# The inverse's results move into the preparation's buffers, and the merge's copies are split between two engines

## The chip, the cores and the metric

The kernel runs on one core of one Trainium2 chip, in one launch. The metric is the device time of a run in microseconds (us). The core's engines are TensorE (PE, with its weight loads apart as PEld), VectorE (DVE), ScalarE (ACT), GpSimd (POOL) and SyncE (SP). Each works through its own list in a fixed order. SP and POOL here mostly issue DMA transfers, in order too.

## The reference

Two layers over 512 latent tokens of width 1024, with 256 context tokens ahead of them. Layer 0 is a bidirectional RWKV-7 recurrence beside a gated short convolution, layer 1 a convolution module. Only the recurrence of layer 0 is touched:

```python
def wkv_scan(S0, r, decay, k, v, kk, a, reverse):
    def step(S, inp):
        r_t, w_t, k_t, v_t, kk_t, a_t = inp
        sa = jnp.einsum("bhvk,bhk->bhv", S, -kk_t)
        S = (S * w_t[:, :, None, :]
             + sa[..., None] * (kk_t * a_t)[:, :, None, :]
             + v_t[..., None] * k_t[:, :, None, :])
        return S, jnp.einsum("bhvk,bhk->bhv", S, r_t)
    S, out = lax.scan(step, S0, (r, decay, k, v, kk, a), reverse=reverse)
    return out, S
...
yac, S_f, S_b = rwkv_seq(rwkv_prep(hc, rc, kc, vc, *rw), zero, zero, r_k, lnx_w, lnx_b, ctx_out)
...
ya, _, _ = rwkv_seq(rwkv_prep(h, r, k, v, *rw), S_f, S_b, r_k, lnx_w, lnx_b, True)
yb = bg * dwconv(cg * xb, sc_w, seg_len)
```

There are 16 heads of 64, both directions, first over the context (whose final states S_f and S_b start the latent scan), then over the latent tokens.

## The kernel before

The scan is done in chunks of 64 tokens. Inside a chunk the dependence of a token on the tokens before it is a unit triangular 64x64 system, one for each head, chunk and direction; its inverse is computed once and then applied by matmuls while the state walks from chunk to chunk.

The work comes in 12 stages, called here c0 to c3 (context, two pairs of heads each, 4 chunk steps) and l0 to l7 (latent, one pair each, 8 chunk steps in both directions). Stage s runs its **chain** (`chain_ctx` or `chain_lat`, the steps from chunk to chunk, each a handful of small matmuls on PE, copies on ACT and, on DVE, the new state H). What belongs to later stages is prepared beside it, in the order that the strings in `STAGE` give; each letter is a part of the program:

- P: projections r, k, v of stage s+2 (big 128x512 matmuls), L: `light`, elementwise work of stage s+2 on DVE and ACT, for direction z=0 and then z=1, in the single buffers `kd`, `a` and `P`;
- H: `heavy` of stage s+2: the triangular blocks (`pa`, masked by DVE into tile E, L601), their copy into `Nt` by ACT (L618), transposes `pb` copied to BKt (L612) and values `pv` copied to UV (L629);
- S: `solve` of stage s+1: DVE transposes `Nt` into X (L650), and runs 31 pairs of operations on X and Y (L656, L658) that invert all 32x32 diagonal blocks. Y is loaded with the unit matrix by a DMA of the POOL queue;
- F, C, O: gate projections, the end of the stage, the short convolution (`conv_branch`) and one product per stage.

The 64x64 inverse is **merged** from the 32x32 ones at the end of `solve`: DVE transposes Y into R1 (L661) and R1 into R2 (L662); ACT copies R1 into E (four copies, L667); PE makes pg, ACT copies it to Gs (L676); PE makes px, ACT copies it into E (L681). R1 is stored in `Nt`, R2 in Y and Gs in X. There is one buffer of each of these, so the next `heavy` can write `Nt`, and the next `solve` can start, only after the merge has read them. The merged part of E is first read in step 0 of the stage's chain (PE, uh<-Ol,E).

All engines' orders are static. They come from a list scheduler that goes by the order in which the program is written, with anchors: `light` and `heavy` are held behind given steps of the chain in progress (`LIGHT_AFTER`, `HEAVY_AFTER`). The big matmuls of projections and gates are spread between the small ones of the chains. Their weights are loaded by SP into two raw buffers, cast by ACT (wh, L126), and DVE makes the remainder (wl, L127). SP also stores the final state of a context chain (h0d<-Hc, L724), between weight loads.

In names, the number is the pair or stage (l4: latent pair 4), and wr, wh and wl are the raw weights, their cast and the remainder.

Of the kernel before, what the change touches and what calls it, by code (L numbers as in the profile page):

```python
# [15 lines left out]
P = 128  # L16
# [15 lines left out]
CONV_AFTER = (0, 2, 7, 6)  # L32
PA_ORDER = ((0, 1), (1, 0), (1, 1), (0, 0))
HEAVY = ("VBOAN", "ANBV")
STAGE = ("OFPLSH", "OSPLHFC")
FILL_R = (0, 0, 2, 3, 4, 4, 4, 4)
FILL_Z = (0, 1, 1, 1, 3, 3, 3, 3)
ZR = (slice(0, 64), slice(64, 128))
# [13 lines left out]
def kernel(ctx: ExitStack, tc: tile.TileContext, I: dict, out: bass.AP):  # L52
    nc = tc.nc
    V, S, G, T = nc.vector, nc.scalar, nc.gpsimd, nc.tensor

    def mm(o, lhsT, rhs, start, stop):
        return T.matmul(o, lhsT, rhs, start=start, stop=stop)  # L57
# [98 lines left out]
    l0, rs = ExitStack(), ExitStack()  # L156
# [20 lines left out]
    def w(tag, name, dt=F32):  # L177
        return wk.tile([P, SIZE.get(tag, 512)], dt, tag=tag, name=name, bufs=NBUF.get(tag, 1))

    def ch3(t, x=CH):  # L180
        return t.rearrange("p (c x) -> p c x", x=x)

    def small(name, shape):
        return cvp.tile(shape, F32, tag=name, name=name)
# [11 lines left out]
    Nt = small("Nt", [P, 16, 32])  # L196
# [196 lines left out]
    def prep_ctx(b, between=None):  # L393
        st = state(False, b)
        for which in (1, 2):
            st["rkv"[which]] = t = w("rkv"[which] + "_", "rkv"[which] + st["nm"])
            for p, cs in st["parts"]:
                project(p, which, t[:, cs])
                if between:
                    between()  # L400
        return st
# [240 lines left out]
    def solve(st):  # L642
        nm, E = st["nm"], st["E"]
        Xt = w("X", "X" + nm)
        X = Xt.rearrange("p (a b) -> p a b", b=32)
        Yt = w("Y", "Y" + nm)
        Y = Yt.rearrange("p (a b) -> p a b", b=16)
        tmp = w("xtmp", "xtmp" + nm)
        nc.gpsimd.dma_start(Y, I["unit"])
        V.transpose(X.rearrange("p (r s) t -> p t r s", r=2),  # L650
                    Nt.rearrange("p q t -> p t q").unsqueeze(2).to_broadcast([P, 32, 2, 16]))
        for i in range(31, 0, -1):
            c0 = i // 2
            m = 16 - c0
            tv = tmp[:, : i * m].rearrange("p (a b) -> p a b", b=m)
            V.tensor_tensor(out=tv, in0=X[:, :i, i : i + 1].to_broadcast([P, i, m]),  # L656
                            in1=Y[:, i : i + 1, c0:].to_broadcast([P, i, m]), op=ALU.mult)
            V.tensor_tensor(out=Y[:, :i, c0:], in0=Y[:, :i, c0:], in1=tv, op=ALU.add)  # L658
        R1 = Nt
        R2 = Yt.rearrange("p (a b) -> p a b", b=32)  # L660
        V.transpose(R1.rearrange("p q (c r) -> p c r q", r=2), Y.rearrange("p (a b) c -> p c a b", a=2))  # L661
        V.transpose(R2, R1)  # L662
        Gs = Xt[:, 0:512].rearrange("p (a b) -> p a b", b=32)
        for z in range(2):
            for b in range(2):
                rs = slice(64 * z + 32 * b, 64 * z + 32 * b + 32)
                S.copy(E[rs, 1 - z, :, 32 * b : 32 * b + 32], R1[rs])  # L667
        pg = px = uhs[1]
        top = [slice(64 * z, 64 * z + 32) for z in range(2)]
        low = [slice(64 * z + 32, 64 * z + 64) for z in range(2)]  # L670
        for q in range(16):
            for z in range(2):
                mm(pg[low[z], q * 32 : q * 32 + 32], E[top[z], 1 - z, q, 32:64], R2[top[z], q, :],
                   True, True)
        for z in range(2):
            S.copy(Gs[low[z]], ch3(pg[low[z]], 32))  # L676
        for q in range(16):
            for z in range(2):
                mm(px[top[z], q * 32 : q * 32 + 32], Gs[low[z], q, :], R1[low[z], q, :], True, True)
        for z in range(2):  # L680
            S.copy(E[top[z], 1 - z, :, 32:64], ch3(px[top[z]], 32))  # L681

    cmm = pinned()

# [176 lines left out]
    def rest(n=1):  # L861
        for g in range(mv["n"], min(mv["n"] + n, 16)):
            half_, kt = g // 8, g % 8
            if kt == 0:
                mv["acc"] = uhs[0] if half_ == 0 else ps.tile([P, 512], F32, tag="zo", name="mpb", bufs=2)
                V.memset(mv["acc"], 0.0)
            for q in range(4):
                u = 4 * half_ + q
                layer, c0 = (0, 2 * D + 512 * u) if u < 2 else (1, 512 * (u - 2))
                if g < 2:  # L870
                    with tc.issue_after(env["last"].ins):
                        nc.sync.dma_start(mws[q], I["mod_w"][layer, kt * P : (kt + 1) * P, c0 : c0 + 512])
                    continue
                nc.gpsimd.dma_start(mws[q], I["mod_w"][layer, kt * P : (kt + 1) * P, c0 : c0 + 512])
            for q in range(4):
                mm(mv["acc"][32 * q : 32 * q + 2, :], s2[:, kt, :], mws[q], kt == 0, kt == KT - 1)
            if kt == KT - 1:
                rested(half_, mv["acc"])
        mv["n"] += n

    def rested(half_, acc):
        row = w("HP", f"mrow{half_}")
        mt = ps_at(f"mr{half_}")
        for b in range(2):
            S.copy(row, acc[:, 256 * b : 256 * b + 256])
            for j in range(2):
                T.transpose(mt[:, (2 * b + j) * P : (2 * b + j + 1) * P], row[:, j * P : (j + 1) * P], ident)
        src = mt.rearrange("p (j q x) -> p q j x", j=4, q=4)[:, :, :, 0]
        for dst, u0, n, bias in (((gate0, 0, 2, col("mod_b0", 16, 8)), (modc1[:, 0:8], 2, 2, col("mod_b1", 0, 8)))
                                 if half_ == 0 else ((modc1[:, 8:24], 0, 4, col("mod_b1", 8, 16)),)):  # L890
            V.tensor_tensor(out=dst.rearrange("p (q j) -> p q j", q=n), in0=src[:, u0 : u0 + n],
                            in1=bias.rearrange("p (q j) -> p q j", q=n), op=ALU.add)
        if half_ == 0:
            V.memset(acc, 0.0)
# [9 lines left out]
    sts = [prep_ctx(0, rest)]  # L904
# [3 lines left out]
    heavy(sts[0])  # L908
    rest()
    solve(sts[0])  # L910
    rest(2)
    sts.append(prep_ctx(1, rest))
    light(sts[1])
# [2 lines left out]
    for s in range(12):  # L916
        st = sts[s]
        if s < 4:
            for i in range(NCTX):
                chain_ctx(st, i)  # L920
        else:
            for i in range(NLAT):
                chain_lat(st, i)
        if s == 11:
            finish(st)
            break
        for x in STAGE[s >= 4]:
            if x == "S":
                solve(sts[s + 1])
            elif x == "O":  # L930
                if sts[s + 1]["lat"]:
                    sts[s + 1]["po"]()
            elif x == "P" and s < 10:
                sts.append(prep_ctx(s + 2) if s < 2 else prep_lat(s - 2))
            elif x == "L" and s < 10:
                light(sts[s + 2], st)
            elif x == "H" and s < 10:
                heavy(sts[s + 2], st)
            elif x == "F":
                fills(s + 1)  # L940
                if s >= 4:
                    finish(st)
            elif x == "C":
                conv_branch(s - 3, st["anchor"])
                if s == 10:
                    rs.close()
                    op = rs.enter_context(tc.tile_pool(name="op", bufs=1, reuse_waits="tile", side="right"))
                    env["lo"] = V
        if s == 3:
            G.memset(cx[:, :, 0:66:65], 0.0)  # L950
            conv_branch(0)
            V.scalar_tensor_tensor(out=gsc1, in0=modc1[:, 8:16], scalar=1.0, in1=col("g_pre1", 0, 8),
                                   op0=ALU.add, op1=ALU.mult)
            gv = ss6
            V.tensor_tensor(out=gv[:, 0:8], in0=gate0, in1=col("g_post", 0, 8), op=ALU.mult)
            V.tensor_tensor(out=gv[:, 8:16], in0=modc1[:, 16:24], in1=col("g_post", 8, 8), op=ALU.mult)
            pgv = ps_at("pgv")
            T.transpose(pgv[:16, :P], gv, ident)
            gvr = w("xtmp", "gvr")[0:16, 0:P]
            S.copy(gvr, pgv[:16, :P])  # L960
            nc.sync.dma_start(gvd.rearrange("a (k p) -> (a k) p", p=P), gvr)
# [26 lines left out]
    with ExitStack() as l1:  # L988
# [118 lines left out]
        for n in range(4):  # L1107
            ws = {}
            for part, tag in ((1, "wa"), (0, "wb")):
                for kt in range(0, KT, 2):  # L1110
# [3 lines left out]
                    w = split(src, f"wc{n}{part}{kt}", tag)  # L1114
# [3 lines left out]
            for m in range(4):  # L1118
# [10 lines left out]
                a = lt("a", f"a{n}{m}")  # L1129
# [20 lines left out]
        for j in range(16):  # L1150
# [5 lines left out]
            t = t2[:, j % 2 * 512 : j % 2 * 512 + 512]  # L1156
# [4 lines left out]
        for j in range(16):  # L1161
# [10 lines left out]
            t = lt("wb" if j < 10 else "xr", f"y{j}", F32R)  # L1172
# [12 lines left out]
        for n in range(2):  # L1185
# [17 lines left out]
            for m in range(4):  # L1203
# [3 lines left out]
                t = lt("a", f"sq{m}{n}") if n else None  # L1207
# [93 lines left out]
```

## Time and profile before

| | before |
|---|---|
| three runs, median | 1486.42 us (1476.52 to 1487.33) |
| the profiled execution | 1487.99 us, of which span 1486.2 us |
| PE busy | 1421.5 us (96%) |
| DVE busy | 955.8 us (64%) |
| ACT busy | 777.6 us (52%) |
| mean granted clock of TensorE | 0.976 of full |

The span is the time from the first to the last recorded instruction; the profiled execution has 1.8 us around it. Context stages lie in about the first 470 us after the start, latent stages from there to about 990 us, and the output projection and layer 1 take the rest, which the change does not touch. A latent stage repeats every 61.8 us (the transposes into R1, L661, start at 649.63, 711.40, 773.21 and 835.16 us).

### The profile page before, as it was taken

Reading aid. Unit: us, or ns where it says so; the run is one execution under the profiler, and the core shown is the slowest. Engines: PE = TensorE matmul, PEld = TensorE weight load, DVE = VectorE, ACT = ScalarE, POOL = GpSimd, SP = SyncE. Lnnn points to the kernel's source line nnn. Section 1 sums busy time; section 2 is a strip of 40 time slices with the busy share of each in tenths; the row PEclk is TensorE's granted clock in tenths of the full one; section 3 lists DMA queues with packets and bytes.
Section 4 is the critical chain, followed back from the end, with each engine's and each line's share of the span. In section 5 each row is a group of like instructions: output and inputs, shape, how many; then the busy total and the mean of one; then the engine's idle time right before and its main releaser. Section 6 shows DMA issues by size and latency. Waiting matters only on the chain.

```text
span 1486.2 us, 29753 instructions
## 1 busy us (share of the span) xinstructions
PE 1421.5 (96%) x11921; PEld 1015.5 (68%) x11921; DVE 955.8 (64%) x2250; ACT 777.6 (52%) x1564; POOL 128.5 (9%) x250
## 2 busy tenths in 40 slices
PE   6899999999999999999999999999889999999998
PEld 1464667878767666666666666677767777688876
DVE  2665576668696978888788787657545535544333
ACT  4536364374755575755757556546544313463222
POOL 2022210000110101011010100011100000000000
PEclk9999997999996999999999999999989999999999
DMA  8754431312232312231222213358603203133322
GB/s 324 216 168 161 154 110 58 103 58 75 74 104 65 90 60 79 62 94 45 86 73 59 90 30 100 131 201 304 208 30 114 86 28 113 46 97 99 98 87 85
DMA packets 137627, 158.55 MB, mean 107 GB/s; under 512 B 15375, under 2 KB 104143, under 8 KB 137369
## 3 DMA queue, kind: packets, MB, share of 16 engines
q1 hardware_dynamic: 121104, 106.47, 23.0%
q0 software_dynamic: 15312, 48.99, 10.3%
q8 instruction: 94, 1.54, 0.4%
q10 hardware_dynamic: 1072, 1.19, 0.2%
q14 instruction: 45, 0.37, 0.1%
HBM read 138.33 MB, written 18.28 MB: 105 GB/s over the span
## 4 chain that ended last, share of the span: by engine, by line
PE 47%; ACT 7%; DVE 5%; issue 1%; DMA 1%; DVEq 0%; SPq 0%; ACTq 0%
PE pu L57 12%; PE f L57 6%; PE pz L57 6%; PE o L57 4%; PE zol L57 3%; PE pbg L57 3%; PE pxb L57 3%; PE uh L57 2%; PE pal L57 1%; PE pc L57 1%; PE px L57 1%; PE pcg L57 1%; ACT Nt L618 1%; DVE E L601 1%; ACT UV L629 1%
## 5 line engine op out<-in xcount | busy, mean ns | idle before, releaser
L57 PE MATMUL o<-wh,y 128*128 128x512 f32 x248 | 80.2, 401 | 1.0 <-ACT wh L126 1.0
L57 PE MATMUL pal<-ARl,BKl 64*128 64x128 f32 x512 | 59.1, 311 | 6.9 <-DVE xtmpc L656 4.3
L658 DVE TENSOR_TENSOR Yl<-Yl,xtmpl 128x126 f32<-128x126 f32 (+22 forms) x248 | 61.9, 250 | 2.2
L656 DVE TENSOR_TENSOR xtmpl<-Xl,Yl 128x126 f32<-128x126 f32 (+22 forms) x248 | 61.9, 249 | 2.0
L57 PEld LDWEIGHTS pal<-ARl,BKl 64*128 64x128 f32 x512 | 44.2, 199 | 26.4 <-DVE E L601 6.1
L1136 ACT CAST ah<-a 64x512 fp32r<-64x512 f32 x32 | 19.8, 618 | 72.9 <-DVE a L1131 72.5
L57 PE MATMUL zol<-UV,E 64*64 64x64 f32 (+1 forms) x1024 | 54.2, 221 | 0.0
L57 PEld LDWEIGHTS o<-wh,y 128*128 128x128 f32 x248 | 46.7, 191 | 10.9 <-ACT wh L126 1.1
L57 PE MATMUL o<-wl,y 128*128 128x512 f32 x124 | 50.3, 405 | 3.9 <-DVE wl L127 3.9
L57 PE MATMUL zol<-Hl,ARl 64*64 64x64 f32 x896 | 50.2, 230 | 1.9 <-DVE Hl L769 1.9
L762 ACT COPY UV<-uh 64x128 f32<-64x128 f32 x128 | 33.4, 261 | 33.4 <-PE uh L57 31.1
L601 DVE TENSOR_TENSOR E<-pal,maskE 128x512 f32<-128x512 f32 x64 | 43.4, 683 | 11.0 <-PE pal L57 10.9
L127 DVE TENSOR_TENSOR wl<-wr,wh 128x1024 fp32r<-128x1024 f32 x28 | 37.0, 1320 | 20.9 <-ACT wh L126 20.7
L57 PEld LDWEIGHTS zol<-Hl,ARl 64*64 64x64 f32 x896 | 35.1, 133 | 20.7 <-issue 16.8
L769 DVE SCALAR_TENSOR_TENSOR Hl<-uh,PCl,HPl 128x64 f32<-128x64 f32 x112 | 26.6, 279 | 30.6 <-PE uh L57 22.6
L57 PEld LDWEIGHTS uh<-UV,BKt 128*64 128x64 f32 x704 | 26.8, 138 | 28.0 <-ACT UV L762 21.6
L57 PEld LDWEIGHTS zol<-UV,E 64*64 64x64 f32 (+1 forms) x1024 | 42.4, 136 | 2.8 <-ACT UV L762 2.1
L1131 DVE TENSOR_TENSOR a<-pu,a 128x512 f32<-128x512 f32 x16 | 11.0, 689 | 51.3 <-PE pu L57 49.0
L1092 DVE SCALAR_TENSOR_TENSOR pr<-px,dbe,What 119x512 f32<-119x512 f32 x32 | 22.5, 746 | 32.8 <-PE px L57 32.7
L126 ACT CAST whcg<-wrcg 128x512 fp32r<-128x512 f32 x16 | 9.9, 619 | 64.0 <-DMA wrcg<-in_ev_w_in_dram 60.1
L126 ACT CAST wh<-wr 128x1024 fp32r<-128x1024 f32 x28 | 29.4, 1049 | 23.5 <-PE o L57 11.0
L57 PE MATMUL uh<-UV,BKt 128*64 128x64 f32 x704 | 37.0, 234 | 4.0 <-ACT UV L762 2.5
(935 smaller groups left out, 4306.5 us busy)
## 6 DMA issues: line engine op xcount, KB each, us to landing
wr<-in_ev_w_out_dram SPq DMA_DIRECT2D x28, 512.0 KB, 5.4
mwo<-in_mod_w_dram POOLq DMA_DIRECT2D x28, 256.0 KB, 3.3
mwr<-in_mod_w_dram POOLq DMA_DIRECT2D x28, 256.0 KB, 4.2
ectx<-in_mod_w_dram SPq DMA_DIRECT2D x12, 512.0 KB, 5.1
wrk<-in_ev_w_in_dram SPq DMA_DIRECT2D x16, 256.0 KB, 2.8
wrv<-in_ev_w_in_dram SPq DMA_DIRECT2D x16, 256.0 KB, 3.7
wrr<-in_ev_w_in_dram SPq DMA_DIRECT2D x16, 256.0 KB, 2.9
wrza<-in_ev_w_in_dram SPq DMA_DIRECT2D x16, 256.0 KB, 2.8
```

What stands on the lines that cost most here:

```text
L57: return T.matmul(o, lhsT, rhs, start=start, stop=stop)
L126: S.copy(hi, raw)
L127: env["lo"].tensor_tensor(out=lo, in0=raw, in1=hi, op=ALU.subtract)
L601: V.tensor_tensor(out=E[:, h, z * NLAT + c0 : z * NLAT + c0 + m, :], in0=pas[h], in1=maskE[:, z * (1 + h) : z * (1 + h) + 1, 0:x].to_broad ...
L618: S.copy(Nt[rs], E[rs, h, :, 32 * b : 32 * b + 32])
L629: S.copy(dst, src if lat or not z else src[:, :, ::-1, :])
L656: V.tensor_tensor(out=tv, in0=X[:, :i, i : i + 1].to_broadcast([P, i, m]), in1=Y[:, i : i + 1, c0:].to_broadcast([P, i, m]), op=ALU.mult)
L658: V.tensor_tensor(out=Y[:, :i, c0:], in0=Y[:, :i, c0:], in1=tv, op=ALU.add)
L762: u_ = S.copy(UV[ZR[1 - h], i : 2 * nch - i : 2 * nch - 1 - 2 * i, ZR[h]], uh[ZR[1 - h], 0:2, :])
L769: h_ = V.scalar_tensor_tensor(out=Hn[:, z, :], in0=uh[:, 2 + z, :], scalar=PC[z][:, i : i + 1], in1=HP[:, z, :], op0=ALU.mult, op1=ALU.add)
L1092: V.scalar_tensor_tensor(out=pr[s][:NPROD], in0=px[s][:NPROD], scalar=dbe[:, 0:1], in1=What[:, n * 512 : n * 512 + 512], op0=ALU.add, op1= ...
L1136: S.copy(ahl[s][hr], a[hr])
```

## The change

The merge becomes a function of its own, `merge`, with a letter M of its own. R1, R2 and Gs no longer lie in `Nt`, Y and X, but in the buffers `kd`, `a` and `P` of `light`. So `Nt`, Y and X are free once the solve's own last operations are through; and the merge of stage s+1 has to come after `light` of stage s+2 is through with those three buffers, while the next `light` has to come after the merge. In `STAGE`, M stands behind L and S, and ahead of H. Of the eight copies of a merge, ACT keeps four and DVE gets four. Instructions on PE, and the DMAs, are the same in number.

```diff
-STAGE = ("OFPLSH", "OSPLHFC")
+STAGE = ("OFPLSMH", "OSPLMHFC")
...
-        R1 = Nt
-        R2 = Yt.rearrange("p (a b) -> p a b", b=32)
+        st["Y"] = Y
+
+    def merge(st):
+        nm, E, Y = st["nm"], st["E"], st["Y"]
+        R1, R2, Gs = (w(t, f"{t}m{nm}")[:, 0:512].rearrange("p (a b) -> p a b", b=32) for t in ("kd", "a", "P"))
         V.transpose(R1.rearrange("p q (c r) -> p c r q", r=2), Y.rearrange("p (a b) c -> p c a b", a=2))
         V.transpose(R2, R1)
-        Gs = Xt[:, 0:512].rearrange("p (a b) -> p a b", b=32)
         for z in range(2):
             for b in range(2):
                 rs = slice(64 * z + 32 * b, 64 * z + 32 * b + 32)
-                S.copy(E[rs, 1 - z, :, 32 * b : 32 * b + 32], R1[rs])
+                (V.tensor_copy if b else S.copy)(E[rs, 1 - z, :, 32 * b : 32 * b + 32], R1[rs])
...
         for z in range(2):
-            S.copy(Gs[low[z]], ch3(pg[low[z]], 32))
+            (V.tensor_copy if z else S.copy)(Gs[low[z]], ch3(pg[low[z]], 32))
...
         for z in range(2):
-            S.copy(E[top[z], 1 - z, :, 32:64], ch3(px[top[z]], 32))
+            (V.tensor_copy if z else S.copy)(E[top[z], 1 - z, :, 32:64], ch3(px[top[z]], 32))
...
     solve(sts[0])
+    merge(sts[0])
...
             if x == "S":
                 solve(sts[s + 1])
+            elif x == "M":
+                merge(sts[s + 1])
```

The order moves in three places of interest. In the order, R1 is called kdm (the buffer kd used by the merge), R2 am and Gs Pm.

The first is ACT between chains l3 and l4, from the merge of l4 to the first scaled output of chain l4 (Ol4, copied from zol4_0). Before:

```order
L667 COPY E100_4343<-Nt_112 32x16x32 x4
L676 COPY Xl4_8086<-uh1_124 32x512 x2
L618 COPY Nt_112<-E110_5045 32x512 x2
L629 COPY UV110_5044<-pvl5_8419 64x8x64 x2
L681 COPY E100_4343<-uh1_124 32x16x32 x2
L618 COPY Nt_112<-E110_5045 32x512 x2
L629 COPY UV110_5044<-pvl5_8419 64x8x64 x2
L789 ACTIVATE gzb4_8634<-pzb4_8609 128x512
L756 COPY Ol4_8642<-zol4_0_8643 128x128
```

And after:

```order
L669 COPY E100_4355<-kdml4_8277 32x16x32 x2
L678 COPY Pml4_8279<-uh1_124 32x512
L683 COPY E100_4355<-uh1_124 32x16x32
L126 CAST whcg50_9336<-wrcg50_9335 128x512
L618 COPY Nt_112<-E110_5060 32x512 x4
L612 COPY BKt110_5061<-pbl500_8406 128x8x64
L612 COPY BKt110_5061<-pbl501_8407 128x8x64
L126 CAST whcg51_9342<-wrcg51_9341 128x512
L612 COPY BKt111_5062<-pbl511_8427 128x8x64
L612 COPY BKt111_5062<-pbl510_8426 128x8x64
L629 COPY UV110_5059<-pvl5_8446 64x8x64 x4
L126 CAST whxb50_9375<-wrxb50_9374 128x512
```

The merge's copies are four in place of eight and stand together ahead of all copies of stage l5's heavy, with whose Nt and UV they were interleaved. Right behind the last row of after come the gate's gzb4 and Ol4, as before.

The second is DVE in the context part, around the state after step 0 of chain c1 (Hc1_0) and the transpose that begins solve c2 (Xc2). Before:

```order
L717 TENSOR_SCALAR Hc1_0_2885<-uh0_123,PCc10_1691 128x64 x2
L717 TENSOR_SCALAR Hc1_0_2885<-uh0_123,PCc11_1721 128x64 x2
L127 TENSOR_TENSOR wlk70_3173<-wrk70_3171,whk70_3172 128x512
L601 TENSOR_TENSOR ectx_121<-pac2001_2842,maskE_108 128x512
L601 TENSOR_TENSOR ectx_121<-pac2000_2841,maskE_108 128x512
L601 TENSOR_TENSOR ectx_121<-pac2101_2862,maskE_108 128x512
L601 TENSOR_TENSOR ectx_121<-pac2100_2861,maskE_108 128x512
L650 STREAM_TRANSPOSE Xc2_3476<-Nt_112 128x32x32
L719 SCALAR_TENSOR_TENSOR Hc1_1_2923<-uh0_123,PCc10_1691,HPc1_0_2918 128x64 x2
```

And after:

```order
L669 COPY ectx_121<-kdmc1_2709 32x16x32 x2
L369 SCALAR_TENSOR_TENSOR lr2_3101<-plr2_3076,hmu_101,lr2_3101 128x511
L127 TENSOR_TENSOR wlk61_3115<-wrk61_3113,whk61_3114 128x512
L678 COPY Pmc1_2711<-uh1_124 32x512
L127 TENSOR_TENSOR wlk70_3179<-wrk70_3177,whk70_3178 128x512
L601 TENSOR_TENSOR ectx_121<-pac2000_2847,maskE_108 128x512
L601 TENSOR_TENSOR ectx_121<-pac2001_2848,maskE_108 128x512
L683 COPY ectx_121<-uh1_124 32x16x32
L601 TENSOR_TENSOR ectx_121<-pac2101_2868,maskE_108 128x512
L601 TENSOR_TENSOR ectx_121<-pac2100_2867,maskE_108 128x512
L650 STREAM_TRANSPOSE Xc2_3482<-Nt_112 128x32x32
L719 TENSOR_SCALAR Hc1_0_2891<-uh0_123,PCc10_1694 128x64 x2
```

The merge of c1 now stands here (it was some 50 rows earlier, ahead of light c2), and Hc1_0 has moved from ahead of heavy c2's masks to behind Xc2, the place where Hc1_1 was. It is the same with merge c2 and Hc2_0 around Xc3. On SP, the stores of h0d from chains c1 and c2 stay ahead of the weight loads wrr30 and wrr50.

The third is PE at the seam from context to latent, ahead of the second half of the triangular blocks of l0 (pal010 and pal011, of direction z=1). Before:

```order
L57 MATMUL plr5_4689<-hlh_118,whr51_4684 128x512
L57 MATMUL plr5_4689<-hll_119,whr51_4684 128x512
L57 MATMUL plr6_4731<-hlh_118,whr60_4720 128x512
L57 MATMUL plr6_4731<-hll_119,whr60_4720 128x512
L57 MATMUL pal0101_4359<-ARl01_4194,BKl01_4195 128x128
```

And after:

```order
L57 MATMUL plr5_4701<-hlh_118,whr51_4696 128x512
L57 MATMUL plr5_4701<-hll_119,whr51_4696 128x512
L57 MATMUL plr5_4701<-hlh_118,wlr51_4697 128x512
L57 MATMUL plr5_4701<-hlh_118,whr51_4696 128x512
L57 MATMUL plr5_4701<-hll_119,whr51_4696 128x512
L57 MATMUL plr5_4701<-hlh_118,wlr51_4697 128x512
L57 MATMUL plr5_4701<-hlh_118,whr51_4696 128x512
L57 MATMUL plr5_4701<-hll_119,whr51_4696 128x512
L57 MATMUL plr5_4701<-hlh_118,wlr51_4697 128x512
L57 MATMUL pal0101_4371<-ARl01_4203,BKl01_4204 128x128
```

With the rows ahead of these, 13 big matmuls of plr5 now stand in a row ahead of pal010, where there were four (two of plr5 and two of plr6).

## Rows read from the trace of the kernel before

**Rows 1.** The page: busy time, share of the span, instructions.

```profile
PE 1421.5 (96%) x11921; PEld 1015.5 (68%) x11921; DVE 955.8 (64%) x2250; ACT 777.6 (52%) x1564; POOL 128.5 (9%) x250
```

**Rows 2.** Windows, two latent stages: us, busy per engine, clock, DMA share, GB/s.

```profile
630.00:692.00 62.00, 59.29 (x774) 40.15 (x774) 51.39 (x154) 40.08 (x95) 7.01 (x13) 1.00 0.25 71
692.00:754.00 62.00, 59.27 (x776) 40.19 (x776) 51.27 (x154) 40.07 (x94) 6.93 (x14) 1.00 0.24 71
```

**Rows 3.** Waits of PE, 692 to 754 us: total, times, longest.

```profile
PE uh L57 <- ACT Ol L756: 0.9, 1, 0.9
PE pzb L57 <- DVE wlzb L127: 0.5, 1, 0.5
...
```

**Rows 4.** Timeline of ACT around merge l4: start, us, instruction, idle before.

```profile
712.53 2.52 ACT L667 COPY E<-Nt 32x512 f32<-32x512 f32 x4 [1.13 <-DVE Nt L661]
715.07 1.17 ACT L676 COPY Xl<-uh 32x512 f32<-32x512 f32 x2
...
718.71 1.17 ACT L681 COPY E<-uh 32x512 f32<-32x512 f32 x2
...
722.83 0.26 ACT L756 COPY Ol<-zol 128x128 f32<-128x128 f32 x1
```

**Rows 5.** Timeline of DVE around the same merge.

```profile
711.40 1.10 DVE L661 STREAM_TRANSPOSE Nt<-Yl 128x512 f32<-128x512 f32 x1
...
721.16 2.01 DVE L650 STREAM_TRANSPOSE Xl<-Nt 128x1024 f32<-128x1024 f32 x1 [1.77 <-ACT Nt L618]
```

**Rows 6.** Groups by line, shapes apart, DVE: busy us, mean ns, idle before.

```profile
L601 DVE TENSOR_TENSOR E<-pal,maskE 128x512 f32<-128x512 f32 x64 | 43.4, 683 | 11.0 <-PE pal L57 10.9
...
L259 DVE TENSOR_SCALAR tok<-tok,ss 128x1024 f32<-128x1024 f32 x6 | 4.5, 753 | 0.2
```

**Rows 7.** Timeline of PE, big matmuls and then a small one.

```profile
705.06 0.40 PE L57 MATMUL pzb<-hll,whzb 128*128 128x512 f32 x1
705.29 0.39 PE L57 MATMUL pzb<-hlh,wlzb 128*128 128x512 f32 x1
705.61 0.27 PE L576 MATMUL pbl<-ident,BKl 64*128 64x64 f32 x1
```

**Rows 8.** Windows of the context part, columns as in rows 2.

```profile
200.00:215.00 15.00, 14.80 (x199) 10.92 (x195) 11.36 (x19) 14.78 (x31) 1.08 (x2) 1.00 0.23 72
215.00:240.00 25.00, 23.80 (x140) 17.66 (x141) 8.78 (x12) 9.87 (x19) 1.07 (x2) 0.59 0.22 64
372.00:384.00 12.00, 12.00 (x192) 9.08 (x193) 9.05 (x21) 9.06 (x19) 4.53 (x8) 0.72 0.37 113
...
440.00:453.00 13.00, 7.47 (x102) 6.00 (x101) 12.19 (x25) 5.12 (x9) 1.66 (x3) 0.74 0.34 101
453.00:470.00 17.00, 17.00 (x159) 12.77 (x156) 4.43 (x10) 7.58 (x15) 0.54 (x1) 0.50 0.12 33
```

**Rows 9.** Waits of PE, 430 to 480 us.

```profile
PE pal L57 <- DVE xtmpc L656: 4.3, 1, 4.3
PE uh L57 <- DVE Yc L662: 1.2, 1, 1.2
```

**Rows 10.** Waits of PE, 200 to 240 us.

```profile
PE plr L57 <- ACT whr L126: 1.2, 1, 1.2
```

**Rows 11.** Timeline of DVE in chain c1: states Hc and the transpose into Xc.

```profile
321.86 0.85 DVE L717 TENSOR_SCALAR Hc<-uh,PCc 128x64 f32<-128x64 f32 x4
...
332.98 2.03 DVE L650 STREAM_TRANSPOSE Xc<-Nt 128x1024 f32<-128x1024 f32 x1 [2.46 <-ACT Nt L618]
334.89 0.83 DVE L719 SCALAR_TENSOR_TENSOR Hc<-uh,PCc,HPc 128x64 f32<-128x64 f32 x4
340.39 0.85 DVE L719 SCALAR_TENSOR_TENSOR Hc<-uh,PCc,HPc 128x64 f32<-128x64 f32 x4
```

**Rows 12.** Timeline of SP's queue at the end of chain c2.

```profile
418.66 1.19 SPq L724 DMA_DIRECT2D h0d<-Hc  x2
419.99 8.90 SPq L123 DMA_DIRECT2D wrr<-in_ev_w_in_dram  x4
```

## Prediction

> **What bounds the kernel now.** I read the page's shares first: PE is busy 96% of the span, DVE 64% and ACT 52% [rows 1]. An average hides stages, so next came the windows. Two successive latent stages look alike: of 62.00 us PE is busy 59.3, DVE 51.3 and ACT 40.1, at full clock [rows 2]. So PE is the bound there; some 2.7 us of a stage are left in which it idles. The waits of PE in one such stage give them names: 0.9 us on ACT's Ol (the first scaled output of a chain), 0.5 on a weight remainder of DVE, the rest in smaller pieces [rows 3]. No wait for the merge itself is among them. In the timeline of ACT the reader sees why Ol is late: from 712.53 us on ACT works without a gap through the merge's copies (2.52, 1.17 and 1.17 us) and those of the next heavy, and reaches Ol at 722.83 [rows 4]. In the context part PE loses more: a wait of 4.3 us for light l0 and 1.2 us for a merge's transposed result [rows 9], 1.2 us for a weight cast behind a full ACT [rows 8, 10], and above all stretches at half clock. At 0.50, the lower of the two levels (1.2 GHz), stand the 17 us from 453 to 470 us; from 215 to 240 us the mean is 0.59, from 372 to 384 us it is 0.72 [rows 8].
>
> **The price of what is moved.** Per merge ACT loses two copies of R1 (2.52/4 = 0.63 us each) and two of PSUM (1.17/2 = 0.585 each): 2 x 0.63 + 2 x 0.585 = 2.4 us [rows 4]. DVE gets these four. The trace has no 32-partition copy on DVE. The nearest rows for a PSUM source are the masks of L601 at 0.683 us for 512 elements; for an SBUF source the scaling of L259, with one source too, takes 0.753 us for 1024, so a 512-element copy lies between 0.38 and 0.683 [rows 6]. The sum is 2 x 0.683 + 2 x 0.38 to 0.683 = 2.1 to 2.7 us per merge; I take 2.3. DVE goes from 51.3 to 53.6 of 62 us, and the 8.4 us left hide it. If that cover were gone, each stage would pay up to 2.7 us.
>
> **Latent stages, seven merges l1 to l7.** The merge moves to an earlier place, and next to it the copies no longer stand among those of Nt and UV. What is removed between Nt and the next solve (Nt, X and Y free early) shortens a DVE wait of 1.77 us [rows 5], which is not on PE's path. What PE can win is its wait on Ol. In the new order ACT still passes four Nt copies, four of BKt, four of UV and the gate ahead of Ol, but 2.4 us less of merge, four of whose copies are done much earlier. The wait can shrink by all of its 0.9 us or by nothing; a weight cast (whxb50) now stands ahead of the gate and Ol, so I take half, 0.45 x 7 = -3.2 us (0 to -6.3).
>
> Against this goes PE's own order. Big matmuls follow each other after 0.23 us, a small one follows a big one after 0.32 [rows 7]: 0.09 us more at a change between kinds. Counted in the order, the changes per stage from pair 0 to 6 go from 61, 61, 63, 63, 63, 63, 53 to 63, 61, 65, 69, 69, 65, 49: +14 in all, 14 x 0.09 = +1.3 us (0 to +3, if the change back costs as much again). And the merge's own matmuls and the bonus product (waiting for the scaled output of the stage before, which on DVE now stands behind the next X of 2.01 us [rows 5]) can bring new waits: 0 to 0.5 us a stage; I take 0.1, +0.7 in all (0 to +3.5). Latent sum: -3.2 + 1.3 + 0.7 = -1.2 us, from -6 to +6.
>
> **The seam from context to latent.** The 4.3 us wait [rows 9] belongs to pal010, which needs the last of light l0. The order puts 13 big matmuls ahead of it where four stood: 9 x 0.23 = 2.1 us of work fall into the gap [rows 7], -2.1 us. Bounds: 0 (if the weights of these matmuls come late) and -4.3. The merge c3 goes behind light l0, which DVE works on here without a gap; its chain starts some rows later, and its 1.2 us wait stays. Weight remainder wlr51 and the four copies also stand on DVE here: I price them at nothing, since PE then has the plr5 matmuls.
>
> **c0 and ACT.** From 200 to 215 us ACT is busy 14.78 of 15.00, with merge c0 in it [rows 8]. Minus 2.4 us of copies, the 1.2 us wait for whr behind it [rows 10] should go: -1.2 us (0 to -1.2).
>
> **Chains c1 and c2.** Their merges now wait for light's last use of the three buffers. Hc1_0 was at 321.86, Hc1_1 behind Xc2 at 334.89, the following step at 340.39 [rows 11]; with Hc1_0 behind Xc2, the chain is one step late, 340.39 - 334.89 = 5.5 us, and chain c2 likewise. PE has projections to fill with, so 0 us; the upper bound is the whole step for both, +11 us. Queued behind are SP's stores of h0d and, in order behind these, weight loads: at chain c2's end the store at 418.66 is followed at 419.99 by four loads wrr [rows 12].
>
> **The sum.** -1.2 - 2.1 - 1.2 = -4.5 us against the profiled execution's 1487.99, so 1483.5. That execution lies 1.6 us above the median of the three runs, 1486.42; against the median the sum gives **1482 us**. The half-clock stretches I leave as they are. In this forecast the terms' own bounds give about 1473 to 1493.
>
> **Rival 1: the clock comes back.** One stretch of half clock began in the gap of 4.3 us: 440 to 453 us, with that gap in it, has a mean of 0.74, and 453 to 470 us 0.50, which costs 13 x 0.26 + 17 x 0.50 = 11.9 us at most (some of the first part is idle anyway). The stretch of 215 to 240 us began after the wait of 1.2 us and costs 25 x (1 - 0.59) = 10 us [rows 8]. If filling the gap, or taking the 2.4 us from ACT, keeps the clock up, the time is 1482 - 12 = 1470 for the first, with both 1460. For it: both stretches start at an idle spot that the change shortens. Against it: from 372 to 384 us PE is busy all of 12.00 us, and the clock still fell to a mean of 0.72 [rows 8], amid the merge's small matmuls, so idle time is not the only thing that brings it down. The Trainium skill, TensorE: Matmul & The Clock Gate, Part 1 (The HAM clock gate), has the clock throttled by default and after an idle stretch, and released by activity; by that rule the shortened gap would win these 12 us, and the stretch of 372 to 384 us, with no idle in it, does not bear the rule out in full.
>
> **Rival 2, slower: late chains starve PE of weights.** Chain c2 ends 5.5 us later, so the store of h0d goes at about 424 and the four loads of wrr come as much later. Those of them that belong to pair 5 feed the 13 matmuls now ahead of pal010. PE would then stand for up to those 5.5 us in place of the gap saved, and a longer idle spell is paid again in clock: another stretch like that of 453 to 470 us, 8.5 to 12 us, at c2 or earlier. It gives 1482 + 2 + 5.5 + 8.5 to 12, about 1498 to 1502. It decides from the point where wrr51's cast is later than plr5's turn. For it: SP's order is strict, and DVE is full at this place. Against it: these loads spread over 8.90 us [rows 12] because they wait for buffers, which does not shift with the store.
>
> **Rival 3: no effect.** The wait on Ol merely becomes one on another copy, since ACT's list up to Ol is as long in the end, and at the seam light l0 ends later by DVE's added work, 2.3 us, which eats the 2.1 gained. Then 1486. Also here: DVE at 53.6 of 62 is no bound, but where it is full already the copies cost.
>
> **How the numbers follow.** Chances: the forecast 0.45; rival 1 0.25 (one stretch 0.15, both 0.10); rival 2 0.15; rival 3 0.15. About 1% (15 us) is what a measurement of this kernel can tell from no change, as its three runs lie 11 us apart. Faster by over 1% is below 1471.6: both stretches (0.10), two thirds of the cases with one (0.10), and the best end of the forecast (0.04): 0.24. Slower by over 1% is above 1501.3: the worse half of rival 2 and its combination with bounds elsewhere: 0.12. Within: 0.64. The range leaves out the lower half of rival 1's two-stretch case and the upper part of rival 2: 1461 to 1499.
>
> **What would show it.** In the profile after: PE's wait on Ol at 0 to 0.9 per latent stage, the transposes into R1 still 61 to 62 us apart; DVE about 53.6 of 62 in such a stage, ACT 37.7; the copies on DVE at 0.38 to 0.68 us. At the seam a wait of pal of about 2 us in place of 4.3, and the same length of half clock behind it. The wait for whr near 215 us gone. Hc1_0 behind Xc2, some 13 us later than before, with no idle of PE around it. A stage period off by more than 1 us, or a half-clock stretch that is gone or new, would make the prediction wrong.

## The result, and the profile after

The changed kernel took 1469.74 us in the median of eight runs (1465.69 to 1473.59), the kernel before 1486.88 (1476.52 to 1494.88). The ratio is 0.9902, 95% interval 0.9875 to 0.9929: 17 us, some 1.2%, less in the difference of the medians. The profiled execution took 1470.48 us, with a span of 1468.7. Forecast were 4.4 us, with 1482 us in a range of 1461 to 1499.

The page after, busy time and share of the span (1468.7 us):

```profile
PE 1417.8 (97%) x11921; PEld 1014.3 (69%) x11921; DVE 987.8 (67%) x2298; ACT 749.9 (51%) x1516; POOL 128.4 (9%) x250
```

Against [rows 1] PE's busy time is 3.7 us less; the other 13.8 us of the span's 17.5 are idle time of PE that went. The mean granted clock is 0.978 after 0.976, so over the whole execution the clock gives almost nothing, though it moves in single stretches, as shown below. DVE has 32.0 us more and ACT 27.7 us less; the 48 copies moved, 12 merges of 2.23 us on DVE, are 26.7 of the 32.0.

To find where the 17.5 us of span went, I set the same events of both traces side by side: the first scaled output of each latent chain (ACT, Ol<-zol) and the states Hc of the context chains. The difference after minus before is a running account:

| event | before | after | difference |
|---|---|---|---|
| chain c0, last state | 260.7 | 251.2 | -9.5 |
| chain c1, first state | 321.9 | 327.4 | +5.6 |
| chain c1, last state | 346.0 | 345.7 | -0.3 |
| chain c2, last state | 418.0 | 420.7 | +2.7 |
| chain c3, last state | 491.5 | 482.6 | -8.9 |
| chain l0 starts | 534.5 | 524.3 | -10.2 |
| chain l1 starts | 599.4 | 586.2 | -13.2 |
| chain l6 starts | 908.5 | 887.5 | -20.9 |
| end of the span | 1486.2 | 1468.7 | -17.5 |

So the context part gains 9.5 us at once, loses 12.2 us of chain time up to the end of c2, and gains 11.6 us at the seam. The stage from l0 to l1 gains another 3.0 us, the stages from l1 to l6 gain 7.7 us, and the rest of the program returns 3.4 us. This account compares one traced execution of each kernel.

**Context part.** Windows of after (us, busy per engine, clock, DMA share, GB/s). All but 300 to 326 and 384 to 402 us are the stretches of [rows 8]:

```profile
200.00:215.00 15.00, 15.00 (x194) 11.67 (x186) 14.19 (x24) 12.91 (x27) 0.55 (x1) 1.00 0.29 89
215.00:240.00 25.00, 24.79 (x260) 18.36 (x259) 16.64 (x40) 14.02 (x30) 2.16 (x4) 1.00 0.35 100
300.00:326.00 26.00, 23.09 (x277) 20.02 (x277) 14.20 (x21) 13.55 (x27) 1.08 (x2) 0.67 0.14 44
...
372.00:384.00 12.00, 11.07 (x98) 7.99 (x96) 10.10 (x17) 11.55 (x24) 4.14 (x8) 1.00 0.26 72
384.00:402.00 18.00, 17.48 (x226) 14.50 (x228) 10.08 (x14) 8.30 (x15) 0.63 (x2) 0.62 0.26 75
...
440.00:453.00 13.00, 9.64 (x117) 7.69 (x117) 12.45 (x25) 5.19 (x10) 2.21 (x4) 0.84 0.34 101
453.00:470.00 17.00, 17.00 (x263) 12.64 (x263) 12.89 (x30) 10.46 (x23) 0.54 (x1) 0.82 0.21 64
```

The reader looks at the clock column. The stretch at 0.59 behind merge c0 is gone (215 to 240 us: 1.00, with 260 matmuls where there were 140), so is the one from 372 to 384 us (1.00 for 0.72), and the one at the seam is less (0.84 and 0.82 for 0.74 and 0.50). Two are new: 300 to 326 us at 0.67 and 384 to 402 us at 0.62; before, both windows had 1.00. In front of each new one PE waits for a merge, as its waits show (296 to 312 us, then 375 to 400 us, then the seam, 440 to 460 us):

```profile
PE pck L57 <- ACT whk L126: 1.4, 1, 1.4
PE uh L57 <- DVE amc L665: 1.4, 1, 1.4
```

```profile
PE uh L57 <- DVE amc L665: 1.4, 1, 1.4
```

```profile
PE pal L57 <- DVE xtmpc L656: 2.1, 1, 2.1
PE uh L57 <- DVE amc L665: 1.1, 1, 1.1
```

The wait for light l0 is 2.1 us in place of 4.3 [rows 9], as forecast. The waits on amc (R2 of a merge) at c1 and c2 are new. So is the wait of 1.4 us on whk, a weight cast that ACT reaches at 304.59 us behind the work of light; it ends 1.3 us before the wait for merge c1 begins. The timeline of DVE shows why PE waits for R2:

```profile
305.01 0.68 DVE L555 SCALAR_TENSOR_TENSOR BKc<-ac,iPc 128x512 f32<-128x512 f32 x1
305.61 1.13 DVE L664 STREAM_TRANSPOSE kdmc<-Yc 128x512 f32<-128x512 f32 x1
306.61 0.72 DVE L367 SCALAR_TENSOR_TENSOR lr<-plr,hmu,lr 128x511 f32<-128x511 f32 x1
307.23 0.71 DVE L665 STREAM_TRANSPOSE amc<-kdmc 128x512 f32<-128x512 f32 x1
307.97 0.85 DVE L669 COPY ectx<-kdmc 32x512 f32<-32x512 f32 x2
```

Light c2's last use of kd and a ends, and at once merge c1 begins, at 305.61 us; before it began at 271.3. Its pg matmuls on PE then wait for R2.

**Latent stages.** Windows from one chain's start to the next, after, and all of PE's waits in the second:

```profile
708.18:768.21 60.03, 59.41 (x773) 40.00 (x772) 54.07 (x158) 37.90 (x91) 6.73 (x12) 1.00 0.25 72
768.21:828.02 59.81, 59.37 (x774) 40.07 (x772) 54.44 (x158) 37.55 (x91) 6.74 (x12) 1.00 0.25 77
```

```profile
PE uh L57 <- ACT UV L764: 0.4, 1, 0.4
```

From chain l3 on, a stage has 60.0 us or less in place of 61.8 to 62.0; the stages from l1 and from l2 still have 61.5 and 60.5. PE is busy nearly as long as before [rows 2]. All five stages from l1 to l6, first before, then after:

```profile
599.40:908.50 309.10, 295.50 (x3863) 201.22 (x3863) 256.22 (x760) 199.18 (x467) 29.56 (x53) 1.00 0.24 70
586.20:887.50 301.30, 297.58 (x3925) 202.29 (x3924) 273.65 (x799) 188.99 (x447) 30.15 (x54) 1.00 0.24 72
```

PE's idle time falls from 13.6 to 3.7 us, and its busy time rises by 2.1 us, all at full clock. Of the waits in [rows 3] those on Ol and on the weight remainder are gone. ACT shows how, around merge l4 and chain l4's first Ol:

```profile
748.16 1.24 ACT L669 COPY E<-kdml 32x512 f32<-32x512 f32 x2
751.26 0.58 ACT L678 COPY Pml<-uh 32x512 f32<-32x512 f32 x1 [1.86 <-PE uh L57]
754.76 0.57 ACT L683 COPY E<-uh 32x512 f32<-32x512 f32 x1 [2.93 <-PE uh L57]
...
763.75 2.36 ACT L629 COPY UV<-pvl 64x512 f32<-64x512 f32 x4 [1.02 <-PE pvl L57]
767.07 0.62 ACT L126 CAST whxb<-wrxb 128x512 fp32r<-128x512 f32 x1 [0.95 <-ACT UV L629]
767.71 0.60 ACT L791 ACTIVATE gzb<-pzb 128x512 f32<-128x512 f32 x1
768.21 0.26 ACT L758 COPY Ol<-zol 128x128 f32<-128x128 f32 x1
```

In [rows 4] ACT came to Ol through ten microseconds without a gap; now it has idle spots ahead of it, and is there when PE wants it.

**The moved copies**, after, by line (min/median/max ns):

```profile
L669 DVE COPY E<-kdml x16: 416/421/424, 515.6 to 913.2; 32x512 f32<-32x512 f32 x16
...
L678 DVE COPY Pml<-uh x8: 696/696/697, 518.3 to 915.1; 32x512 f32<-32x512 f32 x8
...
L683 DVE COPY E<-uh x8: 689/689/690, 521.6 to 918.7; 32x512 f32<-32x512 f32 x8
```

2 x 0.421 + 0.696 + 0.689 = 2.2 us per merge, against 2.3 estimated from [rows 6].

### The profile page after: what moved, and what is told of

Same layout as the page of the kernel before. It is cut to its first block, busy times and chain, and to the rows that moved or that the text cites. A ratio compares the mean times of both kernels' runs of the same rounds, so it can differ in the third digit from the quotient of the medians.

```text
span 1468.7 us, 29754 instructions
## 1 busy us (share of the span) xinstructions
PE 1417.8 (97%) x11921; PEld 1014.3 (69%) x11921; DVE 987.8 (67%) x2298; ACT 749.9 (51%) x1516; POOL 128.4 (9%) x250
## 3 DMA queue, kind: packets, MB, share of 16 engines
q0 software_dynamic: 15312, 48.99, 10.2%
## 5 line engine op out<-in xcount | busy, mean ns | idle before, releaser
L57 PEld LDWEIGHTS uh<-Ol,E 64*64 64x64 f32 x512 | 19.9, 133 | 22.8 <-ACT Ol L758 12.7
```

## The experiments

The theory after reading both traces (A in the texts below): the latent stages win because the merge's copies leave the place ahead of Ol; the context wins behind merge c0 because ACT is relieved, and loses because the buffers kd, a and P tie merges c1 and c2 to the end of light. The rival (B): the relief of ACT does all of it, wherever the merge stands. A third reading (C), that the context loses with any change of its buffers, or that the clock fell by chance in the executions compared, is tried beside them. All versions keep the computation. Each was timed in five rounds beside the kernel before on the same chip; that kernel's median was 1484.7 to 1486.1 us there.

**All copies on ACT, merge as in the change.**

```diff
-                (V.tensor_copy if b else S.copy)(E[rs, 1 - z, :, 32 * b : 32 * b + 32], R1[rs])
+                S.copy(E[rs, 1 - z, :, 32 * b : 32 * b + 32], R1[rs])
...
-            (V.tensor_copy if z else S.copy)(Gs[low[z]], ch3(pg[low[z]], 32))
+            S.copy(Gs[low[z]], ch3(pg[low[z]], 32))
...
-            (V.tensor_copy if z else S.copy)(E[top[z], 1 - z, :, 32:64], ch3(px[top[z]], 32))
+            S.copy(E[top[z], 1 - z, :, 32:64], ch3(px[top[z]], 32))
```

> The merge in the new place and buffers, but all eight copies on ScalarE as before. Theory A (the new place of the merge wins the latent stages, 1.5 to 2 us each, and the copies that left ScalarE win the stretch behind merge c0): the stage period of the latent part stays near 60 us, but the wait for whr and the half clock at 217 us come back, which costs about 10 us; time about 1478 to 1482. Theory B (the copies that left ScalarE do it all): latent period back at 61.8 us, time 1485 to 1488.

Measured: 1474.8 us, ratio 0.9936 (0.9905 to 0.9968). The latent period is 59.8 to 60.0 us from l1 on, so the new place and buffers are enough there without the split, and B fails. But in the traced execution the half clock behind merge c0 did not come back, though ACT kept its copies:

```profile
215.00:240.00 25.00, 24.75 (x259) 18.32 (x259) 17.01 (x33) 16.18 (x35) 2.16 (x4) 1.00 0.32 99
```

So in this execution the split was not needed for it, against A. More can't be said: the twelve runs took 1467.99 to 1483.99 us at a mean clock of 0.983 to 0.973, the traced one 1472.17 at 0.980, and what the longer ones had behind merge c0 is not recorded.

At the seam the split does matter. Without it PE's order has four big matmuls ahead of pal010, as before, its wait is 4.5 us, and half clock follows as in [rows 8]:

```profile
PE pal L57 <- DVE xtmpc L656: 4.5, 1, 4.5
```

```profile
440.00:453.00 13.00, 12.97 (x167) 9.98 (x167) 6.38 (x16) 5.21 (x9) 0.54 (x1) 0.50 0.30 91
```

**Copies split, merge at its old place and in the old buffers.** The merge is called at the end of `solve` and takes `Nt`, Y and X:

```diff
+        if True:
+            merge(st, Xt, Yt)
...
-        R1, R2, Gs = (w(t, f"{t}m{nm}")[:, 0:512].rearrange("p (a b) -> p a b", b=32) for t in ("kd", "a", "P"))
+            R1, R2, Gs = Nt, Yt.rearrange("p (a b) -> p a b", b=32), Xt[:, 0:512].rearrange("p (a b) -> p a b", b=32)
```

> The copies split as in the change, but the merge at its old place and in Nt, Y and X. Theory A: latent period 61 to 61.8 us, no half clock at 217 us (-10 us), and no stall of the late chains c1 and c2; time 1474 to 1480. Theory B: all of the gain, about 1470, with a latent period near 60 us.

Measured: 1459.26 us, ratio 0.9827 (0.9790 to 0.9864): faster than the change by some 10 us, and better than either expectation. The split by itself is worth about 25 us; the new buffers, added to it, take 10 back. The latent period is 60.4 to 60.5 us in most stages, so the split alone also suffices for most of that gain. PE's waits on ACT's Ol, 4.9 us in all before, come to 0.5 us with all copies on ACT and to none here.

**Old buffers in the context only**, and **old buffers in the latent part only.** The condition of the edit above becomes `not st["lat"]`, and `st["lat"]`.

> Copies split everywhere; context merges at the old place and in the old buffers, latent merges as in the change. Theory A: the waits of TensorE for the late merges c1 and c2 and the two half-clock stretches behind them (309 to 325 and 387 to 401 us) go, the latent stages keep 60 us: 1455 to 1465. Theory B, or if the two stretches are not due to the late merges: 1468 to 1472.

> Copies split everywhere; context merges as in the change, latent merges at the old place and in Nt, Y and X. Theory A: latent period back at 61 to 61.8 us, first chain of the latent part still some 10 us earlier than before: 1474 to 1480. Theory B: 1468 to 1472.

Measured: 1457.49 us, ratio 0.9815 (0.9776 to 0.9855), with old buffers in the context; 1475.07 us, ratio 0.9940 (0.9911 to 0.9969), with old buffers in the latent part. The first was run once more and gave 1456.02 us:

> The version with old context buffers and the latent merges of the change once more, beside the other run on the same chip: 1455 to 1461.

The two differ from the change only in one part each: the context's new buffers cost some 12 to 14 us (1469.74 against 1457.49 and 1456.02), the latent part's new buffers win some 2 (1459.26 against 1457.49) to 5 us (1475.07 against 1469.74). The intervals of these last two pairs overlap, so the latent part's share is only likely, though the traces point the same way: the stages l1 to l6 take 303.0 and 302.9 us with the old latent buffers, 301.5 and 301.3 with the new. The context's share is clear. The stretches with new half clock in the change, in the version with old context buffers:

```profile
300.00:326.00 26.00, 26.00 (x318) 21.12 (x317) 17.34 (x36) 18.17 (x43) 0.54 (x1) 0.98 0.12 36
...
384.00:402.00 18.00, 17.70 (x225) 13.39 (x223) 13.13 (x39) 10.37 (x25) 1.08 (x2) 1.00 0.19 53
```

Both are at full clock or nearly. Chain l0 starts at 509.7 us, 14.6 us ahead of the change.

The version with old buffers in the latent part has the context of the change, and warns against tying each stretch to one wait. PE waits 1.4 us for merge c2 there too, at 384.6 us, and no half clock follows; at the seam the wait is 2.1 us as in the change, and the clock is lower than in the change, 0.50 for 0.82 from 453 to 470 us:

```profile
384.00:402.00 18.00, 16.33 (x298) 13.31 (x296) 14.24 (x24) 11.81 (x24) 1.64 (x3) 1.00 0.28 86
...
453.00:470.00 17.00, 17.00 (x140) 11.79 (x139) 10.56 (x28) 9.18 (x20) 0.00 (x0) 0.50 0.19 59
```

**New context buffers without the tie.** In the context the merge is called at the end of `solve` again; R1 and R2 go into the buffer O, which no context chain uses, Gs into X.

```diff
-            R1, R2, Gs = Nt, Yt.rearrange("p (a b) -> p a b", b=32), Xt[:, 0:512].rearrange("p (a b) -> p a b", b=32)
+            om = w("O", f"Om{nm}")
+            R1, R2 = (om[:, 512 * k : 512 * k + 512].rearrange("p (a b) -> p a b", b=32) for k in range(2))
+            Gs = Xt[:, 0:512].rearrange("p (a b) -> p a b", b=32)
```

> As the change, but the context merges put R1 and R2 into the buffer O, which no context stage uses, and Gs into X: new buffers without a tie to light. Theory A (the context loses only by the tie of kd, a and P to light): TensorE has no wait for a transposed merge at 300 to 310 and 380 to 390 us, the merge of c1 begins at about 260 us in place of 305, time 1453 to 1462. Theory C (any change of the context's buffers costs, or what was measured with old context buffers was the chip's clock by chance): 1466 to 1475.

Measured: 1457.18 us, ratio 0.9812 (0.9760 to 0.9864). New buffers as such show no cost (and freeing `Nt` and Y early wins nothing there that these runs can tell). What costs is the late place behind light. C fails by the times of all runs: the change and the two versions with its context buffers and order took 1465.69 to 1483.99 us in 32 runs; this version, the one with all old buffers, the one with old context buffers in both its runs, and the next one took 1452.85 to 1461.29 in 30.

**The four copies out of PSUM stay on ACT** (with old context buffers), so that DVE has two copies per merge.

```diff
-            (V.tensor_copy if z else S.copy)(Gs[low[z]], ch3(pg[low[z]], 32))
+            S.copy(Gs[low[z]], ch3(pg[low[z]], 32))
...
-            (V.tensor_copy if z else S.copy)(E[top[z], 1 - z, :, 32:64], ch3(px[top[z]], 32))
+            S.copy(E[top[z], 1 - z, :, 32:64], ch3(px[top[z]], 32))
```

> As the version with old context buffers (1457.5 us), but VectorE takes only the two copies of R1 into E; the four copies out of PSUM stay on ScalarE. If each copy that leaves ScalarE counts: the time rises by a third to a half of the split's worth, 1462 to 1472. If only the order around the merge matters (theory A for the latent stages): latent period 59.8 to 60.5 us, 1455 to 1462.

Measured: 1458.65 us, ratio 0.9816 (0.9769 to 0.9864): no difference that these runs can tell. Two copies of R1 off ACT are as good as four copies, two of which take DVE 0.69 us each.

**Only merge c0's copies split**, all else as before.

```diff
-                (V.tensor_copy if b else S.copy)(E[rs, 1 - z, :, 32 * b : 32 * b + 32], R1[rs])
+                (V.tensor_copy if b and nm == "c0" else S.copy)(E[rs, 1 - z, :, 32 * b : 32 * b + 32], R1[rs])
...
```

> The kernel before, with only the copies of merge c0 split. If the 1.2 us wait behind merge c0 is what lets the clock fall at 217 us: first state of chain c0 at about 233 us in place of 241.6, no half clock from 217 to 238 us, and most of that kept to the end, 1474 to 1480. If the fall has another cause, or what is won is lost again at the later stretches: 1483 to 1488.

Measured: 1476.62 us, ratio 0.9938 (0.9909 to 0.9967). From l1 on the latent period is 61.7 to 62.0 us, as before, so the latent stages win by the split, or the new place, of their own merges. The first state of chain c0 is at 233.0 us, 8.6 us earlier than before, and the clock stays up behind the merge, where [rows 8] had 0.59:

```profile
215.00:240.00 25.00, 24.62 (x248) 18.05 (x246) 17.46 (x43) 12.97 (x28) 2.17 (x4) 1.00 0.35 106
```

Four copies, 2.4 us of ACT, brought 9.5 us (1476.62 against a median of 1486.13), and the difference is kept to the end: chain l0 starts at 524.3 us in place of 534.5. That median stands for runs that differ: five of the 22 of the kernel before took 1475.66 to 1478.72 us on that chip, at a mean clock of 0.984 to 0.986, as this version does. The seam is not touched by this, and its wait is 4.3 us as before:

```profile
PE pal L57 <- DVE xtmpc L656: 4.3, 1, 4.3
```

**Merge, and with it solve, ahead of light in the context**, in the buffers of the change.

```diff
-STAGE = ("OFPLSMH", "OSPLMHFC")
+STAGE = ("OFPSMLH", "OSPLMHFC")
```

> As the change, with its buffers, but in the context the solve and merge are written ahead of light (M ahead of L): light of stage s+2 waits for merge s+1 in place of the reverse. If the late place of merges c1 and c2 is the loss: their transposes at about 260 and 355 us, 1455 to 1465. If the tie to light costs in either order: light c2 and c3 come later, TensorE waits for their blocks, 1466 to 1480.

Measured: 1470.78 us, ratio 0.9903 (0.9868 to 0.9938), no better than the change. But the account is another one: chain l0 starts at 506.4 us, 18 us ahead of the change, and the stage from l0 to l1 then takes 77.6 us in place of 61.9. The string for the context also orders what is written behind chain c3, and there it puts merge l0 ahead of light l1. So one more version has the order only behind chains c0 to c2:

```diff
-        for x in STAGE[s >= 4]:
+        for x in "OFPSMLH" if s < 3 else STAGE[s >= 4]:
```

> As the change, but the merges of c1, c2 and c3 (written behind chains c0, c1 and c2) stand ahead of light; only behind chain c3 does light l1 stay ahead of merge l0, as in the change. The run with the merge first everywhere had its first latent chain at 506.4 us, the earliest of all, and then lost 15.8 us in the stage from l0 to l1, which had 77.6 us in place of 61.8. If that loss is light l1 waiting for merge l0, that stage is back at 62 us and the time is 1453 to 1460. If the loss belongs to the merges ahead of light as such, it stays at 1466 to 1475.

Measured: 1451.97 us, ratio 0.9781 (0.9732 to 0.9830), the fastest of all, and 4 us under the version with old context buffers on the same chip (1454.15 to 1456.57 there, 1450.55 to 1457.23 here: the ranges overlap). The stage from l0 to l1 has 67.6 us, so most of the 15.8 us is back, not all of it. With the merge ahead of light, then, the borrowed buffers cost the context nothing: it is the order that costs. Its stretches of the context:

```profile
215.00:240.00 25.00, 24.79 (x260) 18.30 (x259) 16.68 (x38) 14.64 (x30) 2.15 (x4) 1.00 0.33 98
300.00:326.00 26.00, 24.89 (x304) 20.07 (x301) 18.20 (x39) 18.55 (x44) 0.54 (x1) 1.00 0.13 38
...
440.00:453.00 13.00, 12.80 (x151) 9.91 (x153) 9.98 (x23) 5.33 (x13) 0.54 (x1) 0.87 0.29 91
453.00:470.00 17.00, 16.68 (x206) 11.86 (x201) 15.63 (x46) 12.86 (x31) 1.21 (x3) 1.00 0.25 73
```

## Why the prediction was right, and where its terms were off

The sign was right and the time lies in the range, but the gain was four times what the sum said. By the prediction's own signs of being wrong its mechanism failed: from l3 on the stage period is some 2 us shorter, and half-clock stretches are gone and new. Term by term:

- **Price of the moved copies:** right. 2.2 us per merge on DVE (2.3 taken), and hidden: DVE has 54.1 to 54.4 of 60 us.
- **Latent stages, -1.2 us:** mis-sized. The account shows -7.7 us from l1 to l6 in five stages, with -3.0 from l0 to l1 ahead of it and 3.4 us given back behind, so -7.3 net. I took half of the wait on Ol, 0.45 us a stage; PE's idle time fell by 2.0 us a stage. The wait on Ol went (0.9 in the stage of [rows 3]; 4.9 us in all before, 0.4 after), the waits on wlzb (0.5) and others with it; how these smaller ones hang together was not tried singly. The charges came too: PE's busy time rose by 2.1 us in these five stages, where +1.3 was charged for changes between big and small matmuls (no run shows that they are the reason), and PE's waits for R2 of latent merges went from 0.7 to 1.4 us. Two runs show that the new place with its buffers (59.8 to 60.0 us) and the split (60.4) each do most of it, so neither is needed for it.
- **The wait for light l0, -2.1 us:** right, 4.3 became 2.1 us, and 4.5 in the version that has four matmuls there again. What rival 1 said of the clock behind it came in part: 440 to 470 us runs at 0.84 and 0.82 in place of 0.74 and 0.50. From the end of c2 to the end of c3 the account shows -11.6 us, which is the wait and this clock together.
- **c0, -1.2 us:** the wait went, and with it the whole stretch at 0.59, the other half of rival 1, 9.5 us. This was the step that failed: I left the half-clock stretches as they were. The run with merge c0 alone split shows that relieving ACT there is enough for the 9.5 us. It does not show that it is needed, since the traced execution with all copies on ACT, but in the new buffers, kept the clock too.
- **Chains c1 and c2, 0 us:** wrong. The mechanism was named (the merge waits for light, the chain is a step late), and its price was put at nothing on the ground that PE has projections to fill with. PE's order is static, and the pg matmuls wait in it: 1.4 us at c1 and at c2, followed in the change by stretches at 0.67 and 0.62. The account loses 12.2 us from c0 to c2, and the runs with old context buffers win 12 to 14 us against the change. The prediction had this as an upper bound, +11 us, and left it out of the bounds of its sum: with it they are about 1475 to 1503, not 1473 to 1493. Hc1_0 came 5.6 us later, not 13, because Xc2 ahead of it came 8.3 us earlier (324.71 us for 332.98).
- **Rivals 2 and 3:** the store of h0d came 2.7 us later (421.37 us for 418.66), and PE shows no wait for a weight at the seam, so rival 2's mechanism showed nothing. Rival 3, no effect, is excluded by the 17 us.

Against the sum of -4.5 us, the change won 13 us more: 8.3 at c0, some 9.5 behind the wait at the seam and 6.1 in the latent stages and behind, less 12.2 at c1 and c2; the rest is 1.3 us between c3 and l0. That what was left out has opposite signs and partly cancels is luck, and it is why the time lies in the range: the versions that split the copies and have only the context merges ahead of light, and so do not pay the 12.2 us, have medians of 1451.97 to 1459.26 us, below it.

The chance of 0.25 for rival 1 was too low: of its two stretches one was won and one shortened, and each of the two new falls has a PE wait ahead of it. The Trainium skill, TensorE: Matmul & The Clock Gate, Part 1 (The HAM clock gate), has the clock throttled by default and after an idle stretch, and released by activity. The traces agree in that shorter waits went with less half clock at c0 and at the seam of the change. Two places do not fit: the fall at 374 us before, with PE busy, and the wait of 1.4 us at 384.6 us in the version with old latent buffers, which no fall follows. These runs explain neither.

## What to carry to other kernels

A buffer that is borrowed to free another ties its new user to the old owner: before borrowing, look at what the owner is doing when the new user wants it, and which of the two goes first, in every part of the program that shares the code (here the latent stages gained perhaps 2 to 5 us, the context stages lost 12 to 14 until the merge went ahead of light). When an engine at 95% busy still shows waits of a microsecond, look at the granted clock behind each of them: a wait of 1.2 us came with 9.5 us. Look at more than one trace before tying a fall to a wait. And a string that orders "the context part" also orders its last stage's hand-over, so its effect there has to be tried apart.

## What was not expected of the hardware

The granted clock of TensorE fell to 0.50 for some 7 to 24 us at a time in the context part (217 to 238 us, 374 to 381 us and 446 to 470 us before, 309 to 326 us and 387 to 401 us after, among others), and the waits ahead of three of these falls were 1.2 to 1.4 us. It did not fall behind every such wait: 1.4 us at 384.6 us in the version with old latent buffers was followed by full clock. The length varied too: behind the same wait for merge c1 the window from 300 to 326 us had 0.67 in the change, 0.64 with old latent buffers and 0.87 with all copies on ACT. The clock also goes with the scatter: on one chip the kernel before spread over 19 us in 11 runs (1476.88 us at a mean clock of 0.985 to 1496.22 at 0.971), two versions without those stretches over 2 and 7 us in six runs each. What exactly makes it fall stays open. A copy of 32x512 elements took DVE 0.42 us from SBUF and 0.69 us from PSUM, ACT 0.62 and 0.58.
